# Row norms by transposed squares and a power on GpSimd, and one index query product moved, in a two-layer decoder trunk

## The chip, the cores and the metric

The kernel runs on one core of one Trainium2 chip. A core has five engines that run their own instruction queues in order and wait for each other by semaphores: TensorE (PE in the profile, its weight loads PEld), VectorE (DVE), ScalarE (ACT), GpSimd (POOL) and SyncE (SP), which here only issues DMAs. TensorE writes its products to PSUM, which has eight banks of 128 x 512 fp32; GpSimd does not read PSUM in this kernel. The metric is the device time of one execution in microseconds (us), the median of several.

## The reference, cut to what matters

A sequence of 512 tokens with 1024 channels goes through two layers. In each, the normalised input feeds one wide projection, four attention branches A to D with a sigmoid gate each, an output projection with a residual, and a SwiGLU block with a residual. One more norm stands at the end. What the change touches are the norms and one of the projection's products:

```python
def rmsnorm(x, g, eps=1e-6):
    xf = x.astype(jnp.float32)
    y = xf * lax.rsqrt(jnp.mean(xf * xf, axis=-1, keepdims=True) + eps)
    return (y * g.astype(jnp.float32)).astype(x.dtype)
...
        h = rmsnorm(x, norm1_g[l])                 # also norm2_g before the SwiGLU block
        p = split_columns(h @ w_in[l])
...     # A, diff_attention, for each of four heads
    o = rmsnorm(o, subln_g) * (1.0 - lam_init)
...     # C, mla_attention
    q = (rmsnorm(c_q, q_norm_g) @ w_uq).reshape(...)
    kv = (rmsnorm(c_kv, kv_norm_g) @ w_ukv).reshape(...)
...     # D, dsa_attention: the indexer
    iq = apply_rope(iq.reshape(B, S, IDX_HEADS, IDX_DIM), icos, isin)
    ik = apply_rope(rmsnorm(ik, ik_norm_g), icos, isin)
        rel = jax.nn.relu(jnp.einsum("bqhd,bkd->bqhk", iqb, ik).astype(jnp.float32))
        idx_score = jnp.einsum("bqh,bqhk->bqk", iwb.astype(jnp.float32), rel)
```

B (native sparse attention) takes values `b_vs`, `b_vw` and gates `b_g` from the projection; the indexer's weights `d_iw` stand beside them.

## The kernel before, in words

Activations lie transposed, channels on partitions and the 512 tokens along a row, so a 1024-channel tensor is eight tiles of 128 x 512. Each fp32 operand is split in two parts that TensorE takes at full rate (`hi` on ACT, `lo`, the rest, on DVE), and a product is three matmuls (`mm3`). Weights stream in 361 pieces of 512 KB (`raw`); each half is split into `wp` by ACT and then DVE, every third one by GpSimd in DVE's place.

The program is written by a planner in Python at build time. The main line issues dense products; every other step is a task, a generator that yields the engine it waits for or a delay (`slack`, `ahead`). The planner keeps its own clock `now` from the matmuls' sizes and a reckoning `busy` for each engine, and after each product (`tick`) runs the tasks that are due. What it thinks due fixes the place of each instruction in its engine's queue, once and for all.

PSUM banks have four tags: three `mm`, two `sc`, two `tr`, one `pv`. The first six products of a layer form one group that fills `mm`, `mm`, `mm`, `sc`, `sc`, `pv` at once: the keys (`c_kr` with `d_ik`), three `c_q`, two `c_kv`. Their post steps (`plain`) multiply the bank by the row of norm factors `R` into `pl` on DVE and free it. Next in the order stand the native values (`native_values`, through `values` and `dense_tokens`, 276 columns: `b_vs`, `b_vw`, gates and `d_iw`), which take `mm`, `mm`, `pv`, `sc`, then four index query products (`iq`, each 8 k-steps x 3 matmuls into one `mm` bank, then rope and a split into `sq`), then gate products. The task `index` scores the queries against the normalised keys (`sk`, `kl`) in `sc` banks, ACT takes the relu (`re`), DVE adds them up (`dm`).

A norm (`rstd`) goes like this: the squares `sq`, already added over tiles, lie with channels on partitions; for each block of 128 tokens TensorE multiplies them with a column of ones, which leaves one column of sums in a `tr` bank; DVE takes 1/sqrt of the 128 x 4 sums (`rsqrt`: a mean, a shift, a first guess `ry` from the bits and three Newton steps `ra`, `ra`, `ry`, twelve instructions); TensorE then transposes each column, broadcast over 128, back to a row. `norm_row` copies that to `R` on ACT; the norms of the keys and of branch A use `rstd` alone. `first_row` is the norm of a layer's input and of the SwiGLU block's, `latent` those of `c_q` and `c_kv` (whose tiles POOL then multiplies by `R`, `pl<-pl,R`), `last` the final one, in two halves of 256 tokens.

Of the kernel before, what the change touches and what calls it, by code (L numbers as in the profile page):

```python
# [11 lines left out]
F32 = mybir.dt.float32  # L12
F32R = mybir.dt.float32r
I32 = mybir.dt.int32
AF = mybir.ActivationFunctionType
ALU = mybir.AluOpType
AX = mybir.AxisListType.X

P = 128
S = 512  # L20
NQ = S // P
# [8 lines left out]
EPS = 1e-6  # L30
# [15 lines left out]
PERM64 = np.array(list(range(8)) + list(range(16, 24)) + list(range(8, 16)) + list(range(24, 64)))  # L46
# [4 lines left out]
def _cols(name, start=0, n=128, perm=None):  # L51
    idx = np.arange(n) if perm is None else np.concatenate([perm + 64 * i for i in range(n // 64)])
    return OFF[name] + start + idx
# [97 lines left out]

PL, LAT, BG, BGS = 1.0, 0.3, 5, 0.5
XR, TD, LD = 1.2, 6, 0.5
LOOK, ZC, NFT, GROUP = 3, 4, 16, 6
NWARM = 9
NKEEP = (NF - NFT) * KT // 4
# [42 lines left out]
class Body:  # L199
# [351 lines left out]
        return k + [kl]  # L551


    def rsqrt(self, ps, n, dim):

        v = self.nc.vector
        x = self.tiny(n, "rx")
        v.tensor_scalar(x, ps, 1.0 / dim, EPS, op0=ALU.mult, op1=ALU.add)
        i = self.tiny(n, "ri")
        v.tensor_scalar(i.bitcast(I32), x.bitcast(I32), 1, None, op0=ALU.arith_shift_right)  # L560
        y = self.sbt([P, n], f"rcol{n}", 4, "ry")
        v.tensor_scalar(y.bitcast(I32), i.bitcast(I32), -1.0, float(0x5F3759DF), op0=ALU.mult, op1=ALU.add)
        for _ in range(3):
            a = self.tiny(n, "ra")
            v.tensor_tensor(a, y, y, op=ALU.mult)
            v.scalar_tensor_tensor(a, a, -0.5, x, op0=ALU.mult, op1=ALU.mult)
            v.scalar_tensor_tensor(y, a, 1.5, y, op0=ALU.add, op1=ALU.mult)
        return y

    def rstd(self, sq, dim, rows=slice(0, P), blocks=range(NQ), slack=1.5):  # L570

        tr, ident = self.nc.tensor, self.ident
        ps = yield from self.bank("tr")
        yield from self.turn()
        for b in blocks:
            tr.matmul(ps[:, b:b + 1], sq[rows, b * P:(b + 1) * P], self.ones[rows, :], start=True, stop=True)
        yield 0.3
        n, b0 = len(blocks), blocks[0]
        col = self.rsqrt(ps[:, b0:b0 + n], n, dim)
        self.rel(ps)  # L580
        yield "v"
        yield slack
        ps = yield from self.bank("tr")
        yield from self.turn()
        for b in blocks:
            tr.transpose(ps[:, b * P:(b + 1) * P], col[:, b - b0:b - b0 + 1].to_broadcast([P, P]), ident)
        yield "p"
        return ps, col

    def norm_row(self, st, dim, n, ahead=0.0, slack=1.5):  # L590
        yield from self.until(lambda: st.get("n") == n)
        yield "v"
        yield ahead
        ps, col = yield from self.rstd(st["s"], dim, slack=slack)
        r = self.u("R")
        self.nc.scalar.activation(r, ps, AF.Copy)
        self.rel(ps)
        return r, col
# [51 lines left out]
    def setup(self):  # L650
        nc, sb = self.nc, self.sb
        self.ident = sb.tile([P, P], F32, name="ident")
        nc.gpsimd.memset(self.ident, 1.0)
        nc.gpsimd.affine_select(out=self.ident, in_=self.ident, pattern=[[-1, P]], base=0, channel_multiplier=1,
                                compare_op=ALU.is_equal, fill=0.0)

        self.kls = [[sb.tile([P, S], F32R, name=f"kl{i}{h}") for h in range(2)] for i in range(2)]
        for kl in self.kls:
            for h in range(2):
                nc.gpsimd.memset(kl[h][64 - 64 * h:128 - 64 * h].bitcast(F32), 0.0)  # L660
        self.ones = sb.tile([P, 1], F32, name="ones")
        nc.vector.memset(self.ones, 1.0)

        self.TM = sb.tile([P, S], F32, name="TM")
        nc.gpsimd.memset(self.TM, 0.0)
        nc.gpsimd.affine_select(out=self.TM[:, S - P:], in_=self.TM[:, S - P:], pattern=[[-1, P]], base=0,
                                channel_multiplier=1, compare_op=ALU.is_ge, fill=BIG)

        self.CM = sb.tile([P, NQ, 32], F32, name="CM")
        nc.gpsimd.memset(self.CM, 0.0)  # L670
        for b in range(NQ):
            nc.gpsimd.affine_select(out=self.CM[:, b, :], in_=self.CM[:, b, :], pattern=[[-16, 32]],
                                    base=b * P - 31, channel_multiplier=1, compare_op=ALU.is_ge, fill=BIG)
        nc.gpsimd.memset(self.CM[:, :, 31:32], BIG)
        self.ZM = sb.tile([P, NQ], F32, name="ZM")
        nc.gpsimd.memset(self.ZM, 1.0)
        nc.gpsimd.affine_select(out=self.ZM, in_=self.ZM, pattern=[[P, NQ]], base=-31, channel_multiplier=1,
                                compare_op=ALU.is_ge, fill=0.0)
# [542 lines left out]
    def latent(self, l, ts, dim, gname):  # L1221

        st, xs = {}, []
        for t in ts:
            x = yield from self.aw(t)
            xs.append(x)
            sq = self.norm_sq(x)
            yield "a"
            self.norm_add(st, sq)
        r, _ = yield from self.norm_row(st, dim, len(ts), 3.0, 8.0)  # L1230
        yield "a"
        out = []
        for i, x in enumerate(xs):
            self.nc.gpsimd.tensor_tensor(x, x, r, op=ALU.mult)
            yield "g"
            out.append(self.task(self.split(x, self.ax(l, gname, i), "lat"), 0))
        return out
# [37 lines left out]
    def mixers(self, l):  # L1275
# [7 lines left out]
        for name, n, dim, g in (("c_q", 3, 384, "qg"), ("c_kv", 2, 256, "kvg")):  # L1283
            ts = [self.win(l, _cols(name, i * P), self.plain) for i in range(n)]
            lat[name] = self.task(self.latent(l, ts, dim, g))
        vv = self.native_values(l)
        iq = [self.rope_to(l, _cols("d_iq", i * P, P, PERM64), self.t_da, self.stack_q) for i in range(4)]
        tix = self.task(self.index(iq, tk, vv), 1, rank=1)
        for z in range(ZC):
            self.gate(l, 2, z)  # L1290
# [10 lines left out]
        for t in range(2):  # L1301
            c = np.concatenate([h * 192 + 128 + PERM_MLA for h in (2 * t, 2 * t + 1)])
# [311 lines left out]
```

## Time and profile before

| | |
|---|---|
| time, median of 3 runs | 2253.92 us (2252.13 to 2255.49) |
| the profiled execution, its own time | 2250.64 us |
| its span, first to last instruction | 2248.4 us |
| TensorE busy | 2199.0 us, 98% |
| VectorE busy | 1402.6 us, 62% |
| ScalarE busy | 929.9 us, 41% |
| GpSimd busy | 655.5 us, 29% |
| mean granted TensorE clock | 0.994 of 2.4 GHz |

The span is what the trace covers; the profiled execution took 2.2 us more and lies 3.3 us under the median. Layer 0 runs from 0 to about 1126 us, layer 1 from there. In the rows, `tr<-ones,sq` are the sums of a norm, `tr<-ident,ry` the transposes back; a name is the written tile, `<-` what it is made from. All instructions show one line of the program, L186, since a helper records them, so they are told apart by tiles.

### The profile page before, as it was taken

How to read it: one execution, taken by the hardware profiler on the slowest of the kernel's cores; microseconds unless marked ns; L12 is line 12 of the kernel's file. 1: busy time of each engine (PE TensorE's matmuls, PEld its weight loads, DVE VectorE, ACT ScalarE, POOL GpSimd, SP SyncE). 2: the span in 40 equal slices, each digit the busy share in tenths (PEclk: the TensorE clock that was granted, in tenths of full speed). 3: DMA queues.
4: the chain of work that ended last, by engine and by line, in shares of the span. 5: the costliest groups of instructions: out<-in, count | busy, mean ns of one | idle time of the engine just before them, and what ended most of it. 6: DMA issues, size and time to landing. Idle time of an engine off the chain costs nothing.

```text
span 2248.4 us, 29760 instructions
## 1 busy us (share of the span) xinstructions
PE 2199.0 (98%) x11089; PEld 1849.3 (82%) x11089; DVE 1402.6 (62%) x2842; ACT 929.9 (41%) x1907; POOL 655.5 (29%) x490
## 2 busy tenths in 40 slices
PE   9899999999999999999999999999999999999998
PEld 7689888788888888888877897887888888888887
DVE  6977898986655533233459778988765564332234
ACT  5456454444443432232334654544443443322233
POOL 2622223421431222122134222334124312322122
PEclk9999999999999999999999999999999999999999
DMA  5222233221223333333433222322222243333322
GB/s 177 82 87 70 72 113 103 80 62 57 77 83 118 111 94 103 93 95 94 130 105 94 75 66 85 114 93 75 58 65 78 82 127 98 95 102 94 103 85 76
DMA packets 61792, 206.55 MB, mean 92 GB/s; under 512 B 6736, under 2 KB 9040, under 8 KB 61648
## 3 DMA queue, kind: packets, MB, share of 16 engines
q1 hardware_dynamic: 61504, 204.45, 29.6%
q8 instruction: 87, 1.43, 0.3%
q14 instruction: 57, 0.47, 0.1%
q10 hardware_dynamic: 144, 0.21, 0.0%
HBM read 200.44 MB, written 4.19 MB: 91 GB/s over the span
## 4 chain that ended last, share of the span: by engine, by line
PE 84%; DVE 11%; issue 2%; ACT 1%; POOL 1%; DMA 0%; SPq 0%; DVEq 0%; POOLq 0%
PE mm L186 72%; PE sc L186 5%; PE pv L186 4%; PE tr L186 3%; DVE wp L186 2%; DVE e L186 1%; DVE sq L186 1%; DVE ra L186 1%; DVE sh L186 1%; DVE sm L186 1%; DVE dm L186 1%; DVE lat L186 1%; DVE sc L186 1%; DVE ry L186 0%; DVE m L186 0%
## 5 line engine op out<-in xcount | busy, mean ns | idle before, releaser
L186 PE MATMUL mm<-h,wp 128*128 128x512 f32 x5136 | 1246.4, 396 | 9.6 <-DVE wp L186 4.3
L186 PEld LDWEIGHTS mm<-h,wp 128*128 128x128 f32 x5136 | 953.2, 189 | 208.5 <-DVE wp L186 5.7
L186 POOL TENSOR_TENSOR wp<-raw,wp 128x512 fp32r<-128x512 f32 x232 | 323.8, 1396 | 1067.8 <-ACT wp L186 1038.4
L186 DVE TENSOR_TENSOR wp<-raw,wp 128x512 fp32r<-128x512 f32 x478 | 400.1, 841 | 180.6 <-ACT wp L186 180.3
L186 ACT ACTIVATE wp<-raw 128x512 fp32r<-128x512 f32 x710 | 423.3, 623 | 182.1 <-PE mm L186 153.1
L186 PE MATMUL mm<-hid,wp 128*128 128x512 f32 x912 | 209.2, 392 | 0.0
L186 PEld LDWEIGHTS mm<-hid,wp 128*128 128x128 f32 x912 | 171.3, 188 | 37.4
L186 ACT ACTIVATE e<-sc,mn 128x128 f32<-128x128 f32 (+1 forms) x192 | 99.2, 524 | 135.1 <-DVE mn L186 135.1
L186 POOL TENSOR_TENSOR sh<-sh,tab 128x512 f32<-128x512 f32 x60 | 81.8, 1363 | 166.5 <-DVE sh L186 166.4
L186 POOL TENSOR_TENSOR z<-z,R 128x512 f32<-128x512 f32 x44 | 57.8, 1315 | 205.6 <-ACT z L186 205.5
L186 PE MATMUL mm<-wp,h 128*128 128x256 f32 (+1 forms) x864 | 115.4, 285 | 0.5 <-DVE ro L186 0.5
L186 DVE TENSOR_TENSOR z<-mm,R 128x512 f32<-128x512 f32 x44 | 30.4, 692 | 126.0 <-PE mm L186 126.0
L186 DVE TENSOR_TENSOR z<-mm,z 128x512 f32<-128x512 f32 x44 | 30.4, 691 | 123.9 <-PE mm L186 123.9
L186 PEld LDWEIGHTS mm<-wp,h 128*128 128x128 f32 x864 | 106.5, 191 | 1.2 <-DVE ro L186 0.7
L186 ACT ACTIVATE pt<-tr 128x384 fp32r<-128x384 f32 (+1 forms) x120 | 62.2, 526 | 99.9 <-PE tr L186 99.0
L186 DVE TENSOR_TENSOR x<-mm,x 128x512 f32<-128x512 f32 (+1 forms) x40 | 23.3, 584 | 122.8 <-PE mm L186 122.8
L186 PEld LDWEIGHTS pv<-pt,v 128*128 128x128 f32 x720 | 93.1, 189 | 7.6 <-issue 2.5
L186 ACT ACTIVATE hid<-z 128x512 fp32r<-128x512 f32 x44 | 27.8, 633 | 161.9 <-DVE z L186 161.9
L186 ACT ACTIVATE z<-z 128x512 f32<-128x512 f32 x44 | 27.9, 634 | 157.6 <-DVE z L186 157.6
L186 PE MATMUL pv<-pt,v 128*128 128x256 f32 x720 | 92.8, 275 | 0.0
L186 DVE CUSTOM_DVE_ANT_0 sc<-sc,TM 128x128 f32<-128x128 f32 (+3 forms) x168 | 78.3, 500 | 16.4 <-PE sc L186 15.6
L186 PE MATMUL mm<-ap,wp 128*128 128x512 f32 x384 | 88.5, 392 | 0.0
(212 smaller groups left out, 2728.9 us busy)
## 6 DMA issues: line engine op xcount, KB each, us to landing
raw<-wstream SPq DMA_DIRECT2D x360, 512.0 KB, 3.6
tab<-tabs SPq DMA_DIRECT2D x16, 256.0 KB, 4.3
x<-xT SPq DMA_DIRECT2D x8, 256.0 KB, 5.5
xr<-xT SPq DMA_DIRECT2D x8, 256.0 KB, 3.9
spill<-x SPq DMA_DIRECT2D x8, 256.0 KB, 2.1
xr<-spill SPq DMA_DIRECT2D x8, 256.0 KB, 3.9
outT<-o SPq DMA_DIRECT2D x8, 256.0 KB, 2.2
raw<-wstream SPq DMA_DIRECT2D x2, 256.0 KB, 3.8
```

The lines of the kernel that those rows point to most:

```text
L186: return f(*args, **kw)
```

## The change

Three edits. The sums: TensorE transposes the blocks of `sq` against the identity (as it already does for other tiles), so that each token's 128 squares lie along a row of the bank, and DVE adds them up in one `tensor_reduce` from PSUM. The root: in place of DVE's twelve instructions GpSimd runs two on the 128 x 4 sums, a scale with an offset and a power with a tile `mhalf` of -0.5; the planner reckons 0.8 us for it and waits for GpSimd, and the delays behind the root are shorter (1.5 to 0.5, for the latents 8 to 4). The order: the first of the four index query products is issued before the native values.

```diff
+POW = 0.8
...
-    def rsqrt(self, ps, n, dim):
-
-        v = self.nc.vector
-        x = self.tiny(n, "rx")
-        v.tensor_scalar(x, ps, 1.0 / dim, EPS, op0=ALU.mult, op1=ALU.add)
-        i = self.tiny(n, "ri")
-        v.tensor_scalar(i.bitcast(I32), x.bitcast(I32), 1, None, op0=ALU.arith_shift_right)
+    def rsqrt(self, x, n, dim):
+
         y = self.sbt([P, n], f"rcol{n}", 4, "ry")
-        v.tensor_scalar(y.bitcast(I32), i.bitcast(I32), -1.0, float(0x5F3759DF), op0=ALU.mult, op1=ALU.add)
-        for _ in range(3):
-            a = self.tiny(n, "ra")
-            v.tensor_tensor(a, y, y, op=ALU.mult)
-            v.scalar_tensor_tensor(a, a, -0.5, x, op0=ALU.mult, op1=ALU.mult)
-            v.scalar_tensor_tensor(y, a, 1.5, y, op0=ALU.add, op1=ALU.mult)
+        self.nc.gpsimd.tensor_scalar(x, x, 1.0 / dim, EPS, op0=ALU.mult, op1=ALU.add)
+        self.nc.gpsimd.tensor_tensor(y, x, self.mhalf[:, :n], op=ALU.pow)
+        self.busy["g"] += POW
+        yield "g"
         return y
 
-    def rstd(self, sq, dim, rows=slice(0, P), blocks=range(NQ), slack=1.5):
+    def rstd(self, sq, dim, rows=slice(0, P), blocks=range(NQ), slack=0.5):
...
-            tr.matmul(ps[:, b:b + 1], sq[rows, b * P:(b + 1) * P], self.ones[rows, :], start=True, stop=True)
+            tr.transpose(ps[:, b * P:(b + 1) * P][:, rows], sq[rows, b * P:(b + 1) * P], ident[rows, rows])
         yield 0.3
         n, b0 = len(blocks), blocks[0]
-        col = self.rsqrt(ps[:, b0:b0 + n], n, dim)
+        sums = ps.rearrange("p (b c) -> p b c", c=P)[:, b0:b0 + n, rows]
+        x = self.tiny(n, "rx")
+        self.nc.vector.tensor_reduce(out=x, in_=sums, op=ALU.add, axis=AX)
         self.rel(ps)
         yield "v"
+        col = yield from self.rsqrt(x, n, dim)
         yield slack
...
-    def norm_row(self, st, dim, n, ahead=0.0, slack=1.5):
+    def norm_row(self, st, dim, n, ahead=0.0, slack=0.5):
...
-        self.ones = sb.tile([P, 1], F32, name="ones")
-        nc.vector.memset(self.ones, 1.0)
+        self.mhalf = sb.tile([P, NQ], F32, name="mhalf")
+        nc.vector.memset(self.mhalf, -0.5)
...
-        r, _ = yield from self.norm_row(st, dim, len(ts), 3.0, 8.0)
+        r, _ = yield from self.norm_row(st, dim, len(ts), 3.0, 4.0)
...
-        vv = self.native_values(l)
-        iq = [self.rope_to(l, _cols("d_iq", i * P, P, PERM64), self.t_da, self.stack_q) for i in range(4)]
+        iq = []
+        for i in range(4):
+            iq.append(self.rope_to(l, _cols("d_iq", i * P, P, PERM64), self.t_da, self.stack_q))
+            if i == 0:
+                vv = self.native_values(l)
```

TensorE's queue at the end of layer 0's first group (the last two rows of that group, `pv_152`, on top), before:

```order
L186 MATMUL pv_152<-h_244,wp_377 128x512
L186 MATMUL pv_152<-h_243,wp_377 128x512
L186 MATMUL tr_461<-ones,sq_446 128x1 x4
L186 MATMUL mm_459<-wp_394,h_142 128x276 x2
L186 MATMUL mm_459<-wp_394,h_143 128x276
L186 MATMUL mm_460<-wp_394,h_142 128x276 x2
L186 MATMUL mm_460<-wp_394,h_143 128x276
L186 MATMUL pv_490<-wp_394,h_142 128x276 x2
```

The same place after the change; between the rows of `mm_444` that are shown stand the other products of that index query (24 matmuls in all):

```order
L187 MATMUL pv_152<-h_244,wp_364 128x512
L187 MATMUL pv_152<-h_243,wp_364 128x512
L187 MATMUL mm_444<-h_142,wp_381 128x512
L187 MATMUL mm_444<-h_143,wp_381 128x512
...
L187 MATMUL tr_451<-ident,sq_433 128x64 x4
...
L187 MATMUL mm_444<-h_244,wp_396 128x512
L187 MATMUL mm_444<-h_243,wp_396 128x512
L187 MATMUL tr_501<-ident,ry_478 128x128 x4
L187 MATMUL mm_509<-wp_413,h_142 128x276 x2
L187 MATMUL mm_509<-wp_413,h_143 128x276
```

The keys' sums (`tr_451`) and the transposes of their roots (`tr_501`) now both stand within the index query product or at its end; the native values (`mm_509` on) follow it.

GpSimd's queue in the same stretch, from the two latents' side of it, before (`rk` is the keys' rope, `kl` their lower part, `wp` a weight half, `pl` a latent tile):

```order
L186 TENSOR_TENSOR sh_566<-sh_566,tab_443 128x512
L186 TENSOR_TENSOR wp_603<-raw_512,wp_603 128x512
L186 TENSOR_TENSOR rk_565<-rk_565,sh_566 128x512
L186 TENSOR_TENSOR wp_699<-raw_556,wp_699 128x512
L186 TENSOR_TENSOR kl_722<-rk_565,sk_692 64x512 x2
L186 TENSOR_TENSOR kl_725<-rk_565,sk_695 64x512 x2
L186 TENSOR_TENSOR wp_803<-raw_675,wp_803 128x512
L186 TENSOR_TENSOR pl_437<-pl_437,R_791 128x512
```

And after the change:

```order
L187 TENSOR_TENSOR sh_523<-sh_523,tab_227 128x512
L187 TENSOR_TENSOR ro_522<-ro_522,sh_523 128x512
L187 TENSOR_TENSOR sh_550<-sh_550,tab_430 128x512
L187 TENSOR_TENSOR wp_593<-raw_481,wp_593 128x512
L187 TENSOR_TENSOR rk_549<-rk_549,sh_550 128x512
L187 TENSOR_SCALAR rx_574<-rx_574 128x4
L187 TENSOR_TENSOR ry_606<-rx_574,mhalf 128x4
L187 TENSOR_SCALAR rx_589<-rx_589 128x4
L187 TENSOR_TENSOR ry_622<-rx_589,mhalf 128x4
L187 TENSOR_TENSOR wp_653<-raw_537,wp_653 128x512
L187 TENSOR_TENSOR kl_706<-rk_549,sk_665 64x512 x2
```

The first index query's rope (`sh_523`, `ro_522`) now stands ahead of the keys' rope, and the roots of the two latents (`rx_574`, `rx_589` and the powers into `ry`) between that rope and `kl`.

## Rows read from the trace of the kernel before

**Rows 1.** The page: busy time of each engine, share of the span, instructions.

```profile
PE 2199.0 (98%) x11089; PEld 1849.3 (82%) x11089; DVE 1402.6 (62%) x2842; ACT 929.9 (41%) x1907; POOL 655.5 (29%) x490
```

**Rows 2.** Waits of PE: total us, times, longest us.

```profile
PE sc L186 <- ACT re L186: 7.1, 5, 3.9
PE pv L186 <- DVE pl L186: 6.3, 2, 3.7
PE tr L186 <- DVE e L186: 5.6, 4, 2.2
PE mm L186 <- DVE wp L186: 4.3, 2, 2.8
PE mm L186 <- DVE IW L186: 3.2, 2, 1.7
```

**Rows 3.** Timeline of PE, first norm: start, us, instruction, count [idle before].

```profile
21.84 0.94 PE L186 MATMUL tr<-ones,sq 128*128 128x1 f32 x8
22.64 1.63 PE L186 MATMUL sc<-h,wp 128*128 128x512 f32 x6
...
26.87 0.60 PE L186 MATMUL tr<-ident,ry 128*128 128x128 f32 x4
27.22 1.63 PE L186 MATMUL sc<-h,wp 128*128 128x512 f32 x6
```

**Rows 4.** Timeline of DVE: first and last of a norm's twelve, two norms.

```profile
22.82 0.16 DVE L186 TENSOR_SCALAR rx<-tr 128x4 f32<-128x4 f32 x1 [0.22 <-PE tr L186]
...
25.00 0.16 DVE L186 SCALAR_TENSOR_TENSOR ry<-ra,ry 128x4 f32<-128x4 f32 x1
...
1171.58 0.15 DVE L186 TENSOR_SCALAR rx<-tr 128x4 f32<-128x4 f32 x1
...
1179.67 1.14 DVE L186 SCALAR_TENSOR_TENSOR ry<-ra,ry 128x4 f32<-128x4 f32 x1
```

**Rows 5.** Timeline, end of layer 0's first group: the keys' sums and the native values.

```profile
41.84 1.05 PE L186 MATMUL tr<-ones,sq 64*128 64x1 f32 x8
42.81 1.02 PE L186 MATMUL mm<-wp,h 128*128 128x276 f32 x6
...
45.78 0.68 DVE L186 TENSOR_TENSOR pl<-pv,R 128x512 f32<-128x512 f32 x1
...
46.51 0.65 PE L186 MATMUL pv<-wp,h 128*128 128x276 f32 x3 [2.67 <-DVE pl L186]
```

**Rows 6.** Stretch: its us, busy PE, PEld, DVE, ACT, POOL, then PEclk.

```profile
47.14:50.55 3.41, 3.41 (x18) 3.41 (x17) 3.41 (x4) 0.95 (x2) 2.31 (x2) 0.50 0.55 154
```

**Rows 7.** Timeline of PE, first index query product behind the native values, both layers.

```profile
66.65 2.58 PE L186 MATMUL mm<-h,wp 128*128 128x512 f32 x10 [1.46 <-DVE wp L186]
...
1181.47 2.56 PE L186 MATMUL mm<-h,wp 128*128 128x512 f32 x10 [2.85 <-DVE wp L186]
```

**Rows 8.** Timeline of layer 0's index scores and what they wait for.

```profile
75.30 1.30 POOL L186 TENSOR_TENSOR wp<-raw,wp 128x512 fp32r<-128x512 f32 x1 [5.86 <-ACT wp L186]
...
96.36 1.28 ACT L186 ACTIVATE sq<-ro 64x512 fp32r<-64x512 f32 x2 [3.69 <-POOL ro L186]
...
98.10 0.50 PE L186 MATMUL sc<-sk,sq 128*128 128x384 f32 x1 [3.87 <-ACT re L186]
```

**Rows 9.** Groups by shape: count | busy us, mean ns | idle us before.

```profile
L186 POOL MEMSET CM<- 128x4 f32 x1 | 0.1, 104 | 0.1
L186 POOL TENSOR_SCALAR_AFFINE_SELECT ZM<-ZM 128x4 f32<-128x4 f32 x1 | 0.6, 575 | 0.1
L186 POOL TENSOR_TENSOR pl<-pl,R 128x512 f32<-128x512 f32 x10 | 16.5, 1662 | 0.0
L186 DVE TENSOR_REDUCE mn<-tr 128x16 f32<-128x512 f32 x2 | 1.4, 692 | 0.1
```

**Rows 10.** Timeline of PE, last norm of the program.

```profile
2238.14 0.58 PE L186 MATMUL tr<-ones,sq 128*128 128x1 f32 x4 [1.52 <-DVE sq L186]
2241.23 0.40 PE L186 MATMUL tr<-ident,ry 128*128 128x128 f32 x2 [2.52 <-DVE ry L186]
```

## The prediction, made before the changed kernel was run

> **What bounds the kernel now.** I read the busy table first, then who TensorE waited for, then the timeline at the longest of those waits. TensorE (PE) is busy for 2199.0 of 2248.4 us [rows 1], so time can only come from work that PE no longer does, from its waits, or from its clock. The other 49.4 us are its waits, start and end among them, and the reader should see that most of the named ones are short waits for VectorE (DVE), in two places: just behind the first group of products of each layer (`pv` waits for `pl`, `mm` for `wp` and `IW`, `sc` for `re`), and in branch A (`tr` for `e`) [rows 2]. The profiled execution took 2250.64 us, 2.2 more than its span and 3.3 less than the median of the runs shown (2253.92). The sum is made against the span; the same 5.5 us (2.2 + 3.3) are added at the end.
>
> **A norm on PE.** There are 20 norms: 18 with four blocks (two in each layer on the whole width, one of the keys, two of the latents, four in branch A) and two with two blocks at the end. Before, four one-column products stand in the trace as eight passes and move PE on by 22.64 - 21.84 = 0.80 us; four transposes with the same identity move it on by 27.22 - 26.87 = 0.35 us [rows 3]. The new sums are such transposes. 16 norms at 0.45 save 7.2 us, the two end halves 0.2 each, and the two of the keys, which took 42.81 - 41.84 = 0.97 [rows 5] and now transpose 64 partitions, about 0.7 each: 9.0 us in all. PE is the bound, so I count this fully. The Trainium skill (TensorE: Matmul & The Clock Gate, Part 4, PE-mode transpose) speaks against it: a transpose takes about 275 ns in a kernel's context. By that four would take 1.1 us and the 16 norms would lose 4.8 us; here four are through in 0.35 [rows 3], and the trace decides.
>
> **A norm's way to its root.** Before, DVE alone runs twelve tiny instructions, from 22.82 to 25.16, so 2.34 us where nothing disturbs it; beside GpSimd (POOL) work the same chain took from 1171.58 to 1180.81, 9.2 us [rows 4]. After, DVE runs one reduction of 512 elements from PSUM, 0.69 us by the nearest row, and POOL two instructions on 128x4. The trace has no power on POOL. Bounds for the two together: 0.2 us if each is like a memset of 128x4, 3.3 us if each is like the dearest POOL group (1.66); a four-element operation that computes took 0.575, so I take 1.15 [rows 9]. With three handovers between engines at 0.2 (PE to DVE took 22.82 - 22.64), the new chain is 0.69 + 1.15 + 0.6 = 2.4 us, about what it was, and up to 1.7 more where POOL is inside another instruction. PE now has 17 to 25 products of 512 columns or as much of smaller ones between sums and roots; 18 such took 26.87 - 22.64 = 4.2 us [rows 3], so 3.9 to 5.3 us. The cover holds, barely in the worst case. The two latent norms of a layer have over 10 us of PE work to hide in. With 3.3 us for the root some 15 norms would wait up to 1 us each.
>
> **The index query product moved ahead of the native values.** Before, the native values take four banks (mm, mm, pv, sc) while the six of the first group are still being emptied. The emptying of the last two stands on DVE behind the keys' twelve-instruction chain; `pv` comes free after 45.78 + 0.68, and PE waits 2.67 us [rows 5]; both layers together 6.3 us [rows 2]. Just behind, PE runs for 3.41 us at a granted clock of 0.50, the lower of its two levels (1.2 GHz) [rows 6]; six such windows stand in the trace, each behind a wait, and each costs half its length, 1.7 us. After, 24 products of one index query come first. They need one mm bank, the first to be freed, and last 24 x 0.235 = 5.6 us; the chain between the emptyings is one 0.69 us reduction. All six banks are free at about 44.8 (46.46 less 2.34, plus 0.69), and the native values begin at about 47.6 (41.84 less 0.45 for the first norm, plus 5.6 and the keys' transposes). So 6.3 + 2 x 1.7 = 9.7 us go. Nothing else is passed: the keys' and latents' sums and their DMAs keep their order, and the rope of this query falls into 48 to 51 us, where POOL has some room (busy 2.31 of 3.41 us [rows 6]).
>
> **What is late next.** In the same stretch PE then waits for a weight half (1.46 and 2.85 us) and for the native values' banks [rows 7], 4.3 + 3.2 = 7.5 us [rows 2]. Both stand on DVE directly behind the two latents' chains. These go (the one in rows 4 alone took 9.2 us; two reductions take 1.4), but the index query's rope and split come ahead (about 4.5 us) and PE arrives some 8 us earlier. I take 5 of 7.5. Then the index scores wait for `re`: ACT's relu stands in its queue behind a split that waits 3.69 us for POOL's rope, and POOL's work there (five latents to scale, the ropes, weight splits) had begun only after 5.86 us of idling [rows 8]. One of the four ropes has left that stretch (two instructions, 3.3 us at most by rows 9), and the latents' scaling starts earlier (their slack falls from 8 to 4) and can fill the idle 5.9, so POOL is done with it some 9 us earlier; PE comes 6 to 9 us earlier (4.9 us a layer of bank wait and clock, up to 3.8 of the 7.5, three norms on PE). Of 7.1 us [rows 2] and two slow-clock windows behind them (3.4) I take 7.
>
> **Branch A and the end.** Here each norm gives DVE 1.6 to 2.6 us back on a queue that PE waits for now and then (5.6 us for `e`, two slow-clock windows), but these waits are not behind a norm's chain directly and the planner's shifted order can add some: 2.5 us, bounds -4 and +9. The last norm is all exposed: 2241.23 - 2238.14 = 3.1 us from the sums to the roots' transposes [rows 10] become 0.2 + 0.35 + 1.15 + 0.6 = 2.3 with half the elements to transpose and reduce; 0.8 us gained (1.7 with the cheap root, 1.4 lost with the dear one).
>
> **Sum.** 9.0 + 9.7 + 5 + 7 + 2.5 + 0.8 = 34.0, less 3 for waits that the new order makes: 31 us. Span 2217.4, median 2223.
>
> **Rivals.** (1) *The start of the layer is held by DVE and POOL, not by the banks.* For it: in that stretch they hand work to each other, and the POOL queue is full; PE's earlier arrival is spent in the next wait. Against it: DVE and POOL both get work away at the right place. Then the waits of rows 7 and 8 stay, and half of the 9.7 is spent there: 9.0 + 4.9 + 0.8 = 15 us, 2239. (2) *The root is dear.* Each roots' transpose is in PE's queue directly, so a late root stops PE. At 1.3 us beside the root, and 4.8 us of PE work on average, a wait begins at a root of 3.5 us, and 15 norms pay each us above it. It eats the 31 us at 3.5 + 31/15 = 5.6 us; at 7 us it costs 15 x 3.5 = 52, and the kernel is 21 us slower than before, 2275. Against it: no POOL group here reaches 1.7 us. The Trainium skill (GPSIMD Engine Reference, section 2.1) gives about 6 us for the first call into freshly loaded code; paid once, at the first norm, it would move the sum by nothing much, and paid at each root it would be this rival. No row here shows either. (3) *The planner's new order gives back what the change takes*, in waits of branches A and B that before fell well: no change, 2252.
>
> **Chances and range.** Forecast 0.61, the held start 0.24, the dear root 0.09, the order 0.06. No change means within 0.2% (4.5 us), about what a measurement of this kernel can tell. Faster than that: the first two, less a little, 0.84; same 0.06; slower 0.10. The forecast's own range is 2210 to 2234; with the held start and the roots' bounds in it, 2208 to 2246.
>
> **What will show it.** Right: 76 transposes of `sq` in the PE rows, four in about 0.35 us; no wait of `pv` for `pl` in either layer; fewer than six windows at clock 0.50; `tr` not waiting for `ry` but at the end; the POOL power under 1.2 us. Wrong: PE's `tr` waiting for POOL's `ry` in most norms (dear root), or `sc` still waiting about 7 us for `re` and `mm` for `wp` (held start).

## The result and the profile after

The changed kernel takes 2225.66 us (median of 4 runs, 2224.95 to 2227.3), the kernel before 2253.53 beside it: a ratio of 0.9874, 95% interval 0.9861 to 0.9887, 27.9 us less. The profiled execution took 2225.23 us with a span of 2223.5; the span of before was 2248.4, so 24.9 us of the gain can be looked for in the two traces. The forecast of 2223 came within 2.7 us. Its reasons were right only in part, and that their sum came out is in part luck, as the experiments show below.

The page after, to be set beside [rows 1]: TensorE has 14.3 us less to do, VectorE 35.4 us less and GpSimd 33.6 us more.

```profile
PE 2184.7 (98%) x11013; PEld 1835.6 (83%) x11013; DVE 1367.2 (61%) x2622; ACT 929.8 (42%) x1907; POOL 689.1 (31%) x530
```

TensorE's waits (total us, times, longest), beside [rows 2]: `pv` for `pl`, `mm` for VectorE's `wp` and `mm` for `IW` are gone; the wait of the index scores (`sc` for `re`), which was to go, has grown from 7.1 to 10.0; the roots on GpSimd are waited for once, at the end.

```profile
PE sc L187 <- ACT re L187: 10.0, 5, 4.9
PE tr L187 <- DVE e L187: 5.0, 3, 2.2
PE mm L187 <- DVE v L187: 2.4, 2, 2.2
PE mm L187 <- POOL wp L187: 2.0, 1, 2.0
PE tr L187 <- POOL ry L187: 1.6, 1, 1.6
```

The first norm, beside [rows 3, 4] (timeline: start, us, engine, instruction, count). Four transposes move TensorE on by 22.33 - 21.98 = 0.35 us, as forecast. One reduction follows on VectorE, then GpSimd's scale and power; the power ends at 25.41, and TensorE comes for it at 27.24.

```profile
21.98 0.60 PE L187 MATMUL tr<-ident,sq 128*128 128x128 f32 x4
22.33 1.63 PE L187 MATMUL sc<-h,wp 128*128 128x512 f32 x6
22.65 0.68 DVE L187 TENSOR_REDUCE rx<-tr 128x4 f32<-128x512 f32 x1
...
23.42 0.56 POOL L187 TENSOR_SCALAR rx<-rx 128x4 f32<-128x4 f32 x1 [16.55 <-DVE rx L187]
...
24.07 1.34 POOL L187 TENSOR_TENSOR ry<-rx,mhalf 128x4 f32<-128x4 f32 x1
...
27.24 0.60 PE L187 MATMUL tr<-ident,ry 128*128 128x128 f32 x4
```

The groups of the root on GpSimd by shape (count | busy us, mean ns): scale and power together are 394 + 1171 ns and a gap of 80, so 1.65 us, where 1.15 was taken.

```profile
L187 POOL TENSOR_TENSOR ry<-rx,mhalf 128x4 f32<-128x4 f32 x18 | 21.1, 1171 | 1.5
...
L187 POOL TENSOR_SCALAR rx<-rx 128x4 f32<-128x4 f32 x18 | 7.1, 394 | 50.7 <-DVE rx L187 50.1
L187 POOL TENSOR_TENSOR ry<-rx,mhalf 128x2 f32<-128x2 f32 x2 | 1.4, 697 | 0.2
```

The end of layer 0's first group, beside [rows 5]: TensorE runs from the index query's first matmuls (3 in the first row, 21 in the third) to the native values without a wait.

```profile
41.43 0.85 PE L187 MATMUL mm<-h,wp 128*128 128x512 f32 x3
42.21 0.46 PE L187 MATMUL tr<-ident,sq 64*128 64x64 f32 x4
42.60 5.09 PE L187 MATMUL mm<-h,wp 128*128 128x512 f32 x21
47.52 0.60 PE L187 MATMUL tr<-ident,ry 128*128 128x128 f32 x4
47.88 1.00 PE L187 MATMUL mm<-wp,h 128*128 128x276 f32 x6
```

Three stretches ahead of the last microseconds run at a granted clock of 0.50, where before had six (both kernels have one more behind the last norm); the stretch of [rows 6] is now at full clock (us, busy PE, PEld, DVE, ACT, POOL, then PEclk). Two of the three lie at the index scores.

```profile
88.06:91.47 3.41, 3.41 (x9) 2.83 (x10) 3.41 (x6) 0.85 (x2) 2.27 (x2) 0.50 0.54 144
309.92:313.34 3.42, 3.42 (x9) 2.56 (x9) 3.28 (x12) 2.23 (x9) 1.45 (x1) 0.50 0.05 10
1193.97:1197.39 3.42, 3.37 (x9) 2.99 (x10) 3.42 (x3) 1.90 (x4) 2.80 (x2) 0.50 0.00 0
47.14:50.55 3.41, 3.41 (x28) 3.27 (x27) 2.53 (x6) 2.27 (x4) 1.95 (x3) 1.00 0.45 159
```

The index scores of layer 0, beside [rows 8]. ACT's relu `re` still stands in its queue behind a split `sq` that waits for GpSimd's rope `ro`. Counted from the start of the last product of a layer's first group, the first scores stand 9.6 us earlier than before in both layers (38.6 us behind it in place of 48.2 in layer 0). So counted, the rope that feeds this split, the third query's, starts some 10 us earlier in layer 0 (43.4 in place of 53.2), as much as TensorE, but only 6 in layer 1 (45.8 in place of 51.8), and there TensorE's longest wait for a relu stands, 4.9 us.

```profile
84.55 1.61 POOL L187 TENSOR_TENSOR ro<-ro,sh 128x512 f32<-128x512 f32 x1
86.19 1.28 ACT L187 ACTIVATE sq<-ro 64x512 fp32r<-64x512 f32 x2 [1.85 <-POOL ro L187]
87.49 0.38 ACT L187 ACTIVATE re<-sc 128x256 f32<-128x256 f32 x1
...
87.93 0.59 PE L187 MATMUL sc<-sk,sq 128*128 128x384 f32 x1 [2.23 <-ACT re L187]
```

The end of the program, beside [rows 10]: 2216.28 - 2214.28 = 2.0 us from the sums to the roots' transposes, where there were 3.1.

```profile
2214.28 0.41 PE L187 MATMUL tr<-ident,sq 128*128 128x128 f32 x2 [1.52 <-DVE sq L187]
...
2216.28 0.43 PE L187 MATMUL tr<-ident,ry 128*128 128x128 f32 x2 [1.58 <-POOL ry L187]
```

**Where the 24.9 us lie.** I followed the start times of TensorE rows that both kernels have. A layer's start, from the last product of its first group (41.5 before, 41.2 after, in layer 0) to the first product that takes a latent (123.3 and 113.5), fell from 81.8 to 72.3 us in layer 0 and from 81.8 to 73.6 in layer 1: 17.6 us. The same products stand in it before and after. The stretch behind it, with branch A in it (up to the last `mm<-oc,wp`), gave 0.6 us in layer 0 and 6.0 in layer 1; from there to the SwiGLU's down product layer 0 lost 1.5 and layer 1 gave 0.2; the ways to the ends of the two first groups (from the program's start, and from layer 0's down product) gave 0.8, and the way from layer 1's down product to the end 1.3. But for rounding that is the whole 24.9.

### The profile page after: what moved, and what is told of

Read it like the earlier page. It is cut to its first block, busy times and chain, and to the rows that moved or that the text cites. A ratio compares the mean times of both kernels' runs of the same rounds, so it can differ in the third digit from the quotient of the medians.

```text
span 2223.5 us, 29420 instructions
## 1 busy us (share of the span) xinstructions
PE 2184.7 (98%) x11013; PEld 1835.6 (83%) x11013; DVE 1367.2 (61%) x2622; ACT 929.8 (42%) x1907; POOL 689.1 (31%) x530
## 4 chain that ended last, share of the span: by engine, by line
PE 86%; DVE 9%; POOL 2%; ACT 2%; issue 1%; DMA 0%; SPq 0%; DVEq 0%; POOLq 0%; ACTq 0%
PE mm L187 74%; PE sc L187 5%; PE pv L187 4%; PE tr L187 3%; DVE wp L187 2%; DVE e L187 1%; DVE sm L187 1%; DVE sh L187 1%; DVE sq L187 1%; DVE sc L187 1%; POOL ro L187 0%; DVE dm L187 0%; ACT wp L187 0%; DVE m L187 0%; POOL sh L187 0%
## 5 line engine op out<-in xcount | busy, mean ns | idle before, releaser
L187 ACT ACTIVATE z<-z 128x512 f32<-128x512 f32 x44 | 27.9, 633 | 156.5 <-DVE z L187 156.5
```

The source lines that it names most:

```text
L187: return f(*args, **kw)
```

## Experiments

Two theories stand against each other. By the prediction the gain is a sum of separable parts: TensorE's shorter passes (9.0), the order (9.7), the shorter VectorE chain (5 and more). The rival is that one thing holds the layer's start, VectorE's twelve-instruction chains, and that the other two are worth little beside it. "Start" in the texts is the stretch of a layer just defined, layer 0 / layer 1; it was 81.8 / 81.8 us before and 72.3 / 73.6 after. Starts and waits are those of the one profiled execution. The kernel before, taken beside each of the kernels below, had medians of 2252.27 to 2253.97 us, so a difference of 2 us between two of them says little; and each edit also changes what the planner sets where. Not run: the root alone on GpSimd, with the sums by ones and the old order.

### The order alone

```diff
-        vv = self.native_values(l)
-        iq = [self.rope_to(...) for i in range(4)]
+        iq = []
+        for i in range(4):
+            iq.append(self.rope_to(...))
+            if i == 0:
+                vv = self.native_values(l)
```

> The kernel before with one edit of three: the first index query product ahead of the native values; sums by ones and roots on VectorE as before. Parts add: the two bank waits of pv for pl (6.3 us) and the two slow-clock windows behind them (3.4 us) go, nothing else: 2253.5 - 9.7 = 2244 us (2241 to 2247), and the waits of mm for wp and IW stay near 7.5 us. Rival, VectorE's chains hold the layer start whatever the order: the waits come back at the next bank or weight, 2250 to 2254.

Measured: 2243.18 us, ratio 0.996 (0.9947 to 0.9974), start 79.5 / 76.7. The size was met, the reason was not: `pv` no longer waits, but within the native values TensorE now waits for the weight half behind the latents' chains, 7.9 us in layer 0 (waits of TensorE).

```profile
PE mm L186 <- DVE wp L186: 11.7, 2, 7.9
```

### The norms alone

The same lines the other way: the changed kernel with the native values first again.

> The changed kernel with the old order: native values first, then the four index query products; sums by transposes, roots on GpSimd. Parts add: 2225.7 + 9.7 = 2235 us (2232 to 2238), with pv waiting for pl 1 to 2.5 us in each layer, since pv is emptied about 1.7 us earlier and TensorE comes 0.5 us earlier. Rival, the shorter VectorE chain alone cures the layer start: no wait over 0.5 us there, 2225 to 2229. Rival, the shorter chain does nothing without the order: 2240 or more, the 9.0 us of TensorE passes and the end alone being gained (2253.5 - 10).

Measured: 2225.47 us, ratio 0.9883 (0.9869 to 0.9896), start 75.4 / 72.1. In time the second reading holds: without the order the whole gain is there. Its "no wait over 0.5 us" holds at the banks only; TensorE waits once for VectorE's `IW`, 2.2 us in layer 0. The timeline of this kernel shows why `pv` is not late. Both `sc` banks are emptied ahead of the reduction, which is 0.42 us long, and `pv` right behind it; TensorE waits 0.16 us.

```profile
40.41 1.38 DVE L187 TENSOR_TENSOR pl<-sc,R 128x512 f32<-128x512 f32 x2
...
42.18 0.42 DVE L187 TENSOR_REDUCE rx<-tr 128x4 f32<-128x256 f32 x1 [0.39 <-PE tr L187]
42.52 0.68 DVE L187 TENSOR_TENSOR pl<-pv,R 128x512 f32<-128x512 f32 x1
...
43.25 0.65 PE L187 MATMUL pv<-wp,h 128*128 128x276 f32 x3 [0.16 <-DVE pl L187]
```

### The root back on VectorE

```diff
-        self.nc.gpsimd.tensor_scalar(x, x, 1.0 / dim, EPS, op0=ALU.mult, op1=ALU.add)
-        self.nc.gpsimd.tensor_tensor(y, x, self.mhalf[:, :n], op=ALU.pow)
-        self.busy["g"] += POW
-        yield "g"
+        v.tensor_scalar(x, x, 1.0 / dim, EPS, op0=ALU.mult, op1=ALU.add)
+        ...  # shift, first guess, three Newton steps as before
+        yield "v"
```

> The changed kernel with the root back on VectorE (the transposed sums are reduced as in it, then the eleven or so tiny VectorE instructions of before in place of GpSimd's scale and power). If the roots' place matters for VectorE's queue: the waits of mm for wp and IW behind the latents' norms come back in part (2 to 5 us) and the end loses 1.2 us: 2230 us (2227 to 2235), relu wait unchanged. Rival, GpSimd's queue is the tight one at the index scores, so that its two small instructions a norm cost more than they relieve: 2220 to 2225, the wait of sc for re shorter by 2 us or more.

Measured: 2246.95 us, ratio 0.9976 (0.9967 to 0.9986), start 79.4 / 79.4: 21.3 us of the gain gone, where I had expected about 4. The timeline of layer 0: two reductions, then a chain in which six of the tiny instructions take 1.1 to 1.2 us, each of them ending 0.02 to 0.03 us behind the end of a GpSimd instruction, and the others 0.15 to 0.17, and behind it the weight half that TensorE has waited 6.67 us for.

```profile
58.28 0.15 DVE L187 TENSOR_SCALAR rx<-rx 128x4 f32<-128x4 f32 x1
58.47 1.15 DVE L187 TENSOR_SCALAR ri<-rx 128x4 int32<-128x4 int32 x1
...
60.81 5.30 POOL L187 TENSOR_TENSOR kl<-rk,sk 64x512 fp32r<-64x512 f32 x4
...
66.37 0.16 DVE L187 SCALAR_TENSOR_TENSOR ry<-ra,ry 128x4 f32<-128x4 f32 x1
66.45 0.69 DVE L187 TENSOR_TENSOR wp<-raw,wp 128x512 fp32r<-128x512 f32 x1
...
67.19 1.52 PE L187 MATMUL mm<-wp,h 128*128 128x276 f32 x5 [6.67 <-DVE wp L187]
```

Of the 21.3 us some 13 lie in the two starts. The granted clock is 0.50 for 23.9 us ahead of the end, where it was for 10.2, and that is about 7 of them.

The delays behind the root are short here, so 8.0 us of waits for `ry` could be theirs. The next kernel has those of before (`slack` 1.5, latents 8.0) and is else the same.

> The root on VectorE once more, with the delays of the kernel before (1.5, and 8 for the latents, in place of 0.5 and 4), so that TensorE's transposes of the roots stand where VectorE's chain can be done. If the short delays made most of the 21 us by which the VectorE root was slower: the 8.0 us of waits for ry go and part of the 17 for wp: 2234 us (2230 to 2238). If VectorE's chains in the queue ahead of the weight splits are the cost, whatever the delays: waits for wp stay over 10 us, 2240 to 2246.

Measured: 2257.76 us, ratio 1.0018 (1.0008 to 1.0027), start 80.7 / 80.7. Both readings of it fell on the size. The waits for `ry` went to 3.1, those for `wp` stayed at 15.8, and branch A got worse (`mm` for `v` 5.8, `tr` for `ec` 4.3). So the root's place counts, not the delays. And against the order alone (2243.18) this kernel is 14.6 us slower (13 by the two ratios). The two differ in the sums, and in one more point between sums and root at which the planner may turn to other work; which of the two costs the time was not tested.

### The sums by ones again, the root on GpSimd

```diff
-            tr.transpose(ps[:, b * P:(b + 1) * P][:, rows], sq[rows, b * P:(b + 1) * P], ident[rows, rows])
+            tr.matmul(ps[:, b:b + 1], sq[rows, b * P:(b + 1) * P], self.ones[rows, :], start=True, stop=True)
...
-        self.nc.vector.tensor_reduce(out=x, in_=sums, op=ALU.add, axis=AX)
+        self.nc.vector.tensor_copy(x, ps[:, b0:b0 + n])
```

> The changed kernel with the sums by products with a column of ones, as in the kernel before (VectorE copies the 128x4 sums out of PSUM in place of reducing 512 elements); roots on GpSimd and the order as changed; nothing moves in memory. If the nine microseconds of TensorE passes are real and at the bound: 2225.7 + 9 = 2235 us (2232 to 2238). Rival, the shorter VectorE instruction (0.2 in place of 0.69 us) pays for it or TensorE's passes are covered: 2226 to 2230.

Measured: 2227.98 us (2226.3 to 2228.39), ratio 0.9892 (0.9877 to 0.9907), start 72.4 / 71.9. Only 2.3 us come back (4 by the two ratios), not 9. TensorE's passes are there: it is busy 7.2 us longer than in the changed kernel, with one slow-clock window fewer (1.7), so 8.9 us of passes.

```profile
PE 2191.9 (99%) x11089; PEld 1843.4 (83%) x11089; DVE 1357.5 (61%) x2623; ACT 929.9 (42%) x1907; POOL 686.7 (31%) x530
```

It waits 6.4 us less in return (span 2224.3, +0.8): `sc` for `re` 6.8 in place of 10.0, for `kl` 1.0 in place of 2.2. The planner also sets some of TensorE's other products in another order: the stretch of the `mm<-oc,wp` rows, with branch A's norms, took 2.8 us less in layer 0 and 4.7 more in layer 1, so this comparison doesn't tell how much of 8.9 - 2.3 is work that fell into old waits and how much is order.

### A dear root, and a tile that moved the weights

```diff
+        for _ in range(3):
+            self.tc.nc.gpsimd.tensor_tensor(self.mspare[:, :n], x, self.mhalf[:, :n], op=ALU.pow)
         self.nc.gpsimd.tensor_tensor(y, x, self.mhalf[:, :n], op=ALU.pow)
...
+        self.mspare = sb.tile([P, NQ], F32, name="mspare")
```

> The changed kernel with three more powers of the same size on GpSimd ahead of each root's own (results thrown away), 3.06 us more for each of 18 roots and 2.1 for the two of the end; the order of all else is the same. From the gaps between the power's end and TensorE's transposes of the roots in the changed kernel's trace (0.05 to 6.3 us) the sum of what stands out is 21 us, in some 15 norms: 2247 us, up to 2258 where the clock falls behind the longer waits. By the prediction's own rule (a wait begins at a root of 3.5 us, 15 norms): root 1.75 + 3.06 = 4.8, so 15 x 1.3 = 20 us. Rival, the cover is deeper than the gaps show, since TensorE has slack elsewhere: under 2235.

Measured: 2288.08 us, ratio 1.0159 (1.0145 to 1.0173), 62 us more than the changed kernel where 21 to 32 were expected. The waits for the roots were as expected, 22.3 us. But every row of 512-column products with `wp` as weights had become longer, far from any norm too. The next three kernels settle that: an unread tile in the same place, one at the front of the memory, and the powers without a new tile (written into `ry`).

> The changed kernel with one more tile of 16 bytes a partition that nothing reads, placed behind mhalf: everything allocated behind it, the weight halves wp among it, moves up by 32 bytes; no instruction but one memset is added. With dear roots, whose added tile moved wp in the same way, every 512-column matmul with wp as its weights took 0.2337 us in place of 0.2297, those without wp the same as before. If the place of wp in memory sets that pitch: 26 us slower than the changed kernel, 2251 us (2247 to 2255). If GpSimd's extra powers did it: 2226 us.

Measured: 2250.16 us, ratio 0.9985 (0.9976 to 0.9995): 24.5 us from 32 bytes that nothing uses. A stretch of SwiGLU at full clock in this kernel (columns as above, matmuls in brackets behind busy PE): 430 matmuls in 100 us.

```profile
900.00:1000.00 100.00, 100.00 (x430) 80.31 (x430) 31.10 (x44) 26.40 (x46) 22.93 (x18) 1.00 0.31 95
```

The same stretch of the changed kernel: 439.

```profile
900.00:1000.00 100.00, 100.00 (x439) 82.05 (x438) 33.97 (x47) 27.68 (x48) 24.39 (x18) 1.00 0.31 93
```

> The changed kernel with an unread tile of 32 bytes a partition at the very front: all the 128x512 tiles and wp move up by 32 bytes together (before and in the changed kernel both stand at 32 past a multiple of 64; here both at 0). If the step between the streamed tile and wp counts: pitch 0.230 and 2226 us. If wp's own place counts (0 past a multiple of 64 being the slow one): 0.234 and 2251 us. If the streamed tile's place counts too, something else, either way.

Measured: 2226.24 us, ratio 0.9881 (0.9864 to 0.9897). The first reading holds: with both moved by 32 bytes the pace is back.

```profile
900.00:1000.00 100.00, 100.00 (x438) 82.06 (x437) 34.06 (x47) 27.84 (x49) 24.01 (x18) 1.00 0.30 95
```

So for these products the step between the streamed tiles and the weights counts, and not where the weights stand. The fourth combination, streamed tiles at 0 and weights at 32, was not run.

> Dear roots again, three more powers on GpSimd ahead of each root, now written into the root's own tile, so that no tile is added and wp stays where it is in the changed kernel. With the pitch back at 0.230: 2288 - 26 = 2262 us (2257 to 2267): 22 us of TensorE waits for the roots, some 11 for weight halves that GpSimd makes late, some for the clock. Rival, the pitch came from the powers: 2288 again.

Measured: 2266.57 us, ratio 1.0055 (1.004 to 1.007). Slower than before, by a mechanism the prediction had named, with a root that took 5.1 us here (4.5 to 6.2 in the 18 norms of four blocks). TensorE waits for the roots 27.0 us; the prediction's rule gives 15 x (5.1 - 3.5) = 24 for this length. It did not name the second wait, 14.8 us for weight halves that GpSimd splits behind the roots. Against the changed kernel these two waits are 38.2 us more, TensorE's busy time, with more of it at the lower clock, is 11.7 more and the other waits are 9.8 less: 40.1 us of span.

```profile
PE mm L187 <- POOL wp L187: 14.8, 2, 8.4
```

### What holds the index scores

Three edits at the wait that the change did not cure. First GpSimd is relieved (`latent` scales its tiles on VectorE):

```diff
-            self.nc.gpsimd.tensor_tensor(x, x, r, op=ALU.mult)
-            yield "g"
+            self.nc.vector.tensor_tensor(x, x, r, op=ALU.mult)
+            yield "v"
```

> The changed kernel with the five latent tiles of a layer scaled on VectorE (0.69 us each) in place of GpSimd (1.66 each), which takes 8.3 us out of GpSimd's queue ahead of the index queries' ropes. If that queue holds the index scores: the wait of sc for re falls from 10.0 to under 5 us and the slow-clock windows behind it go with it, 2225.7 - 7 = 2219 us (2215 to 2222). Rival, ScalarE's or VectorE's own queue holds them: the wait stays over 8 us, or comes back as mm or sc waiting for VectorE, 2224 to 2232.

Measured: 2226.88 us, ratio 0.9889 (0.9872 to 0.9905), the wait 10.4 us, start 73.2 / 73.3. GpSimd's load alone is not what holds it. The work went to another feeder of the same stretch, though: GpSimd is idle now, but it waits for VectorE's part of the rope (`sh`), and ScalarE's split for GpSimd.

```profile
90.73 1.28 POOL L187 TENSOR_TENSOR sh<-sh,tab 128x512 f32<-128x512 f32 x1 [2.73 <-DVE sh L187]
...
93.71 1.28 ACT L187 ACTIVATE sq<-ro 64x512 fp32r<-64x512 f32 x2 [5.91 <-POOL ro L187]
```

Then the latents' delay (`norm_row(st, dim, len(ts), 3.0, 8.0)` in place of `4.0`):

> The changed kernel with the latents' delay behind the root back at 8 in place of 4. The prediction's step (the latents are scaled earlier, so GpSimd is done with them earlier, so the index scores wait less) would make it slower: wait of sc for re 14 us or more, 2230 to 2234. The other reading (the same GpSimd work stands ahead of the ropes either way, and the shorter delay only puts the scaling ahead of ropes that could have gone first): wait the same or shorter, 2220 to 2227.

Measured: 2225.69 us (2223.93 to 2229.34), ratio 0.9885 (0.9871 to 0.99), the wait 7.0 us, start 71.5 / 74.1 (in an execution of 2229.34 us, the longest of the four). No difference in time that can be told; no gain of the shorter delay shows.

Last, ScalarE's queue:

```diff
+    def late_q(self, r):
+        yield 4.0
+        return (yield from self.stack_q(r))
...
-            iq.append(self.rope_to(l, _cols("d_iq", ...), self.t_da, self.stack_q))
+            iq.append(self.rope_to(l, _cols("d_iq", ...), self.t_da, self.late_q))
```

> The changed kernel with one more planned delay: 4.0 between an index query's rope on GpSimd and its split on ScalarE, so that in ScalarE's queue the relus of the scores that are already computed (re, four of them in place of one) stand ahead of the split of the third query, which waits for GpSimd's rope. If the index scores wait because a relu stands in ScalarE's queue behind a split that is not yet fed, whoever feeds it: the wait of sc for re falls from 10.0 to under 4 us and the two slow-clock windows there go, 2225.7 - 6 - 3 = 2217 us (2214 to 2221). Rival, the whole chain of that stretch is late (the scores then wait for the splits themselves, sc for kl or sq): 2223 to 2228.

Measured: 2230.05 us, ratio 0.9902 (0.9886 to 0.9919), start 77.2 / 73.6. The wait of `sc` for `re` did fall, to 4.4 us, and the kernel got 4.4 us slower: the delay holds for all four queries, and the first one's split on VectorE, at 56.99 in the changed kernel, now stands at 67.49, right ahead of the emptying of the native values. TensorE waits there, 8.7 us in the two layers together. In layer 1 the one wait fell from 4.9 to 0.7 us, the other came with 4.5, and the start is the same. So what ScalarE's queue alone is worth this kernel doesn't tell.

```profile
67.49 3.34 DVE L187 SCALAR_TENSOR_TENSOR sq<-ro,sq 64x512 fp32r<-64x512 f32 x2
...
71.53 0.21 DVE L187 TENSOR_SCALAR IW<-mm,ry 128x8 f32<-128x8 f32 x1
...
71.89 2.47 PE L187 MATMUL mm<-h,wp 128*128 128x512 f32 x5 [4.22 <-DVE IW L187]
```

No kernel tried beats the changed one; the norms without the order, the longer delay, the shifted memory and the latents on VectorE lie within 1.3 us of it.

## Why the prediction was right or wrong

- **The norm on TensorE (9.0).** As work it is right (8.9 us of passes). The step "PE is the bound, so I count this fully" failed: with the other edits in place it moved the time by 2.3 us (4 by the ratios), since TensorE, earlier by it, waited more. With the chain on VectorE the kernel with transposed sums was even 14.6 us slower.
- **The way to the root.** The order of size was right: 0.68 on VectorE and 1.65 on GpSimd where 0.69 and 1.15 were taken; the power's mean is 1.17, within the 1.2 named, though 7 of 18 took 1.33 to 1.50. In the cover, 25 products at the 0.235 used are 5.9 us, not 5.3; nothing hangs on it. The cover holds: the smallest gap between a power's end and TensorE's transposes was 0.37 us, but for the last norm.
- **The order (9.7).** In the changed kernel the waits and the two slow-clock windows went as said. Alone the order gave 9.1 us, though its wait for `wp` grew from 4.3 to 11.7. But the step "all six banks are free at about 44.8" failed: with the short reduction they are free at 43.20 without the order. It left out that the second `sc` bank would be emptied ahead of the reduction (0.6), that a reduction of the keys takes 0.42 in place of 0.69, and that TensorE's sums themselves are done some 0.7 earlier. The order then adds nothing that can be measured. Either edit cures this wait; I counted it for the one and gave the other only what came after.
- **The waits for `wp` and `IW` (5 of 7.5).** 2.0 remain, so 5.5; mechanism and size right. This and the term before are the same cause, VectorE's chain: moved back, it costs 21 us, some 13 of them in the two starts. The prediction gave the shorter chain 8.3 us in all (5, 2.5 and 0.8); the norms without the order gave 26.8.
- **The index scores (7).** Wrong: the wait grew by 2.9 us and both windows stayed. The step that failed is "POOL is done with it some 9 us earlier; PE comes 6 to 9 us earlier". Counted as above, TensorE came 9.6 us earlier in both layers, GpSimd's rope 10 in layer 0 but 6 in layer 1; where both come earlier by the same, the wait stays, and even by the step's own figures no more than 3 us a layer would have gone. Relieving GpSimd, or the longer delay, left the time as it was; a relu stands behind a split in ScalarE's queue, and when that was changed the stretch waited elsewhere. What holds the stretch at about 72 us stays open.
- **Branch A and the end (2.5 and 0.8).** The end gave 1.1. The stretches with branch A gave 6.0 in layer 1 and 0.6 in layer 0, which lost 1.5 behind it; the kernel with the sums by ones moved them by 3 to 5 us either way, so why they moved is not shown.
- **Rivals.** The held start was half true: the start was held by VectorE's chains, which the change took away, and some of TensorE's earliness was spent at the index scores. The allowance of 3 us for new waits is about what that cost. The dear root is real, but the change's root is far from it with 1.65 us. It decides earlier than at the 5.6 us that were named: at 5.1 the kernel is slower than before (2266.57), since the rule left out the weight halves behind the roots. The 6 us for a first call into fresh code that the Trainium skill (GPSIMD Engine Reference, section 2.1) gives do not show here: the first power took 1.34, 0.08 us behind the scale.
- **The sum.** 34.0 less 3 against 27.9 looks close, but 25.7 of the 34.0 (9.0, 9.7 and 7) were put down to parts that, with the others in place, moved 2 to 4 us, nothing that can be measured, and the wrong way. The root's place, which was given 8.3, moved 21. That these errors cancel is luck.

## What to carry over

Tiny instructions on a full queue cost what stands behind them, more than their own length: before counting passes saved on the bounding engine, look whose queue the feeders stand in. When two edits remove the same wait, price each with the other in place; a sum of parts can be right with the parts wrong. And when an experiment adds a tile, compare the pace of untouched products first.

## What the hardware showed

- **The place of the weights.** 512-column products with weights in `wp` took 0.230 us with the streamed tiles and `wp` both 32, or both 0, past a multiple of 64 bytes, and 0.234 with the one at 32 and the other at 0: 24.5 us of 2226, at the same granted clock. Products without `wp` kept their pace, also those of `rp` with the 32 columns of `KC` as weights, whose place moved by the same step (0.231 both times); so the step alone is not the whole rule.
- **A power on GpSimd.** 128x4 took 1.01 to 1.50 us, 128x2 0.70: even the cheapest of four elements a row costs more than two.
- **VectorE beside GpSimd.** In the chain shown above, six of twelve instructions of 128x4 took 1.11 to 1.22 us in place of 0.16 while GpSimd ran operations of 128x512 and 64x512; integer ones as well as products. The reduction from PSUM that the change puts in their place does not grow so: in the changed kernel six of 128x512 ran all or most of their time beside such GpSimd operations and took 0.68 to 0.69 us, as the others did.
